# A two-layer hybrid transformer on one core: buffering of the modulation weights, a call's delay before their dots, and the place of one operand of a seven-product matrix multiplication

## The chip, the core and the metric

The kernel runs on one core of one Trainium2 chip. Five engines of the core work side by side: TensorE (PE; its weight loads are PEld), VectorE (DVE), ScalarE (ACT), GpSimd (POOL) and SyncE (SP), which here issues nearly all DMAs. Each engine takes its own instructions in order and waits at semaphores for the others. The metric is the device time of one execution in microseconds (us); below 1 us, nanoseconds (ns) are used.

## The reference

There are two streams of 256 tokens with 1024 channels, `h_lat` and `h_ctx`, and two layers. A layer is a half feed-forward block (ffn), a mixer (attention in layer 0, an mLSTM in layer 1), and a second ffn. What scales, shifts and gates each block comes from two conditioning vectors `c` and `c_ctx`, through a 1024 x 9216 matrix in each layer:

```python
def half_ffn(h, shift, scale, gate, w_in, w_out, g, b):
    xm = modulate(h, shift, scale)
    a, u = jnp.split(xm @ w_in, 2, axis=-1)
    y = (jax.nn.silu(a) * u) @ w_out
    return post_norm(h, 0.5 * gate * y, g, b)
...
    for i in range(DEPTH):
        mod_lat = jnp.split((jax.nn.silu(c) @ ada_w[i] + ada_b[i])[:, None, :], N_MOD, axis=-1)
        mod_ctx = jnp.split((jax.nn.silu(c_ctx) @ ada_w[i] + ada_b[i])[None, None, :], N_MOD, axis=-1)
        h_lat = half_ffn(h_lat, mod_lat[0], mod_lat[1], mod_lat[2], ffn_w_in[i, 0], ffn_w_out[i, 0], ln_g[i, 0], ln_b[i, 0])
        h_ctx = half_ffn(h_ctx, mod_ctx[0], mod_ctx[1], mod_ctx[2], ffn_w_in[i, 0], ffn_w_out[i, 0], ln_g[i, 0], ln_b[i, 0])
...
```

`w_in` is 1024 x 5632 and `w_out` is 2816 x 1024, all in float32. The last layer needs only `h_lat` after its mixer.

## The kernel before

**Precision.** A float32 operand x is split into a high part (ACT copies it to the type fp32r) and a low part (DVE subtracts the high part from x); `split` (L221) issues the two. A product is then three matmuls (`mm3`, L236): high by high, high by low, low by high. The stationary operand (weights) is 128 x 128; the moving operand (tokens) has 256 or 512 columns.

**An ffn** (`ffn`, L658) has two halves of 11 units each. An in-unit j (`unit_in`, or `fast_in` where the cheap form is used) multiplies all tokens by 128 columns of the `a` half of `w_in` and 128 of its `u` half; `ffn_g` (L547) makes silu(a)*u (an ACT Silu, L568, and a DVE product, L569) and splits it. After a half's units come the out-units d (`unit_out`, L681): eight of 33 matmuls with 512 columns in half 0, then four more such and four split by stream (the tail) in half 1; each ends in DVE additions to h (L692). The first four units (LEAD) of an ffn are done stream by stream with 256 columns. Weights arrive by SP's queue into three `raw` buffers (L206, issue at L207) and are split into one of seven `w` buffers (`pair`, L210), each 2 x 1024 values and 64 more, so that the pair may be shifted by `sh` values.

**The cheap form.** In the second half (hf 1) of the two middle ffns, (layer 0, second) and (layer 1, first), `fast_in` (L606) does a unit by seven half-size products instead of eight (a Winograd-Strassen scheme over the 2 x 2 blocks of the weights and of the two token streams). The seven products are a11, a12, s1, s2, a22, s4, s3, each of 12 matmuls with 256 columns: 84 matmuls a unit, 924 for the 11 units. Three sums of tokens, `made[0]`, `made[1]`, `made[2]`, are made beforehand by `fast_sums` (L579) after out-units 4 and 5 of half 0. They stand in one tile (`fast_operands`, L572): `made[0]` and `made[1]` at multiples of 1024 values, and `made[2]` pushed by FLIP = 56 values (224 bytes), so that it does not begin on a multiple of 64 values (256 bytes). All weights of the cheap form stand at SH = 16 values past such a multiple. Only the product a22 (L646) reads `made[2]`.

**The modulation matrix** is taken in pieces of 128 output columns, (layer, dt), dt = 0 to 71, 512 KB each. `ada_load` (L327) sends a piece to one of two `ada` buffers (SP, L331); `ada_dot` (L334) multiplies it by a conditioning vector and sums, a DVE instruction over 128 x 1024 (L337). A piece takes one dot for each stream that needs it: two for pieces 0 to 39 of layer 1, one for 40 to 71. `ada` (L343) does the load and then its dots. The 72 pieces of layer 1 are spread over the two middle ffns: `side` (L1598) gives the ffn functions to call after units, and `some(n)` (L1604) takes pieces until n dots are covered. `DOTS` (L91) says how many: in ffn (0, 1) four dots after each in-unit of half 0, three after out-units 0 to 3 of half 0, two after those of half 1; in ffn (1, 0) three, two and three. The calls of the four LEAD units come together after the fourth (L717). Dots are pinned (`pin`, L406): pinned instructions of an engine keep the order of the program among themselves, as do the two residual steps (L543) after every in-unit. Everything else on an engine is ordered by the scheduler that builds the program, earliest code first.

**Pools.** The ada buffers and the two silu'd conditioning vectors (`cb`) live in a pool `cp` at the right end of SBUF, opened by `silu_all`. Before out-unit 4 of half 0 (SUMSAT, L739) the pool is closed and its place given to the pool `st` with the token sums; after the last cheap unit `st` is closed and a new `cp` opened (L736).

Of the kernel before, what the change touches and what calls it, by code (L numbers as in the profile page):

```python
# [9 lines left out]
F32 = mybir.dt.float32  # L10
F32R = mybir.dt.float32r
# [7 lines left out]
P = 128  # L19
# [3 lines left out]
TL = 256  # L23
# [4 lines left out]
NFH = 11  # L28
# [3 lines left out]
BLOCK = 64  # L32

SH = 16
# [9 lines left out]
WB = 7  # L44
# [43 lines left out]

SUMSAT = 4
FLIP = 56  # L90
DOTS = {  # L91
    1: {("in",): 4, ("out", 0): 3, ("out", 1): 2},
    2: {("in",): 3, ("out", 0): 2, ("out", 1): 3},
}

TAILSTEP = {(0, 3, 1): 'bmccccccc', (1, 0, 2): 'c', (1, 0, 6): 'v', (1, 1, 7): 'rxxxxxxxx'}
# [73 lines left out]
class Body:  # L170
# [98 lines left out]
    def setup(self):  # L269
        nc, a = self.nc, self.a  # L270
        self.cols = col = self.t([P, 3 * BLOCK // 2])
        for i, x in enumerate((1.0, 1.0 / D, 1.0 / (D - P), 0.5 / D)):
            nc.vector.memset(col[:, i : i + 1], x)
        self.mean1, self.half = col[:, 1:2], col[:, 3:4]
        self.ones, self.mean, self.most = (col[:, i : i + 1].broadcast_to([P, P]) for i in range(3))

        self.h = self.t([P, ND, T])
        self.xh = self.t([P, ND, T + BLOCK], F32R)
        self.xl = self.t([P, ND, T + BLOCK], F32R)
        self.ident = self.t([P, P])  # L280
        self.vec = self.t([P, V_N])
        self.mod = {}
        self.s1 = {}

    def silu_c(self):

# [40 lines left out]
    def ada_load(self, layer, dt):  # L327
        if (layer, dt // ND) not in self.mod:
            self.mod[layer, dt // ND] = self.t([P, 2, ND])
        r = self.t([P, 1024], tag="ada", bufs=2, pool=self.cp)  # L330
        self.nc.sync.dma_start(r, self.a["ada_w"][layer, dt])  # L331
        return r

# [9 lines left out]
    def ada(self, layer, dt, vecs=(0, 1)):  # L343
        r = self.ada_load(layer, dt)
        for v in vecs:
            self.ada_dot(r, layer, dt, v)

    def modv(self):
        return self.t([P, 2, ND], tag="modv", bufs=12)
# [222 lines left out]
    def fast_operands(self, st):  # L572

        n = ND // 2 * TL
        x = self.t([P, 6 * n + FLIP], F32R, pool=st)
        at = [2 * i * n + (FLIP if i == 2 else 0) for i in range(3)]
        self.made = [[x[:, a + p * n : a + (p + 1) * n].rearrange("p (k f) -> p k f", f=TL) for p in range(2)] for a in at]

    def fast_sums(self, i):  # L579

# [22 lines left out]
        V.scalar_tensor_tensor(d, a, -1.0, d, ALU.mult, ALU.subtract)  # L603
        self.split(d, *made(2))

    def fast_in(self, j, w_in, st):  # L606

        nc, V, S = self.nc, self.nc.vector, self.nc.scalar
        half = 4 * P
        r0, r1 = (self.raw(w_in[2 * j + i]) for i in range(2))  # L610
        sums = self.t([P, 4 * half], tag="sums", bufs=1, pool=st)
        part = lambda x, i: x[:, i * half : (i + 1) * half]
        a11, a21, a12, a22 = part(r0, 0), part(r0, 1), part(r1, 0), part(r1, 1)
        s1, s2, s4, s3 = (part(sums, i) for i in range(4))
        add = lambda o, x, y: V.tensor_tensor(out=o, in0=x, in1=y, op=ALU.add)  # L615
        ws = [self.pair(sh=SH, n=half)] + [self.pair(sh=SH) for _ in range(3)]
        self.split(a11, *ws[0])
        self.split(r1, *ws[1])
        add(s1, a21, a22)
        add(s2, s1, a11)  # L620
        self.split(sums[:, : 2 * half], *ws[2])
        add(s4, s2, a12)
        add(s3, a11, a21)
        self.split(sums[:, 2 * half :], *ws[3])
        w = {n: [part(x, i) for x in ws[p]] for n, p, i in (
            ("a11", 0, 0), ("a12", 1, 0), ("a22", 1, 1), ("s1", 2, 0), ("s2", 2, 1), ("s4", 3, 0), ("s3", 3, 1),
        )}
        of = lambda k0, g: lambda k: self.x(k0 + k, g)
        made = lambda i: lambda k: [x[:, k, :] for x in self.made[i]]

        def product(o, name, x, first, last):
            for k in range(ND // 2):
                c = slice(k * P, (k + 1) * P)
                self.mm3(o, [y[:, c] for y in w[name]], x(k), first and k == 0, last and k == ND // 2 - 1, group=False)

        x, yv, z = self.mm()[:, :TL], self.mm(), self.mm()[:, :TL]
        y, v = yv[:, :TL], yv[:, TL:]
        a, u = self.tmp(), self.tmp()
        product(x, "a11", of(0, LAT), True, False)
        S.copy(a[:, :TL], x)  # L640
        product(y, "a12", of(ND // 2, LAT), True, True)
        product(v, "s1", of(0, CTX), True, False)
        S.copy(u[:, TL:], v)
        product(x, "s2", made(0), False, False)
        S.copy(a[:, TL:], x)
        product(z, "a22", made(2), True, True)  # L646
        S.copy(u[:, :TL], z)
        product(v, "s4", of(ND // 2, CTX), False, True)
        V.tensor_tensor(out=a, in0=a, in1=yv, op=ALU.add)
        S.activation(a, a, AF.Silu)  # L650
        product(x, "s3", made(1), False, True)
        u2 = u.rearrange("p (n f) -> p n f", n=2)
        V.scalar_tensor_tensor(u2, x[:, None, :].broadcast_to([P, 2, TL]), -1.0, u2, ALU.mult, ALU.subtract)
        V.tensor_tensor(out=a, in0=a, in1=u, op=ALU.mult)
        gh, gl = self.gt[j] = tuple(self.t([P, self.gw], F32R, tag=k, bufs=self.gn, pool=self.gp) for k in ("gh", "gl"))
        self.split(a, gh, gl)

    def ffn(self, layer, s, gate, groups, side, start=None, cpool=None):  # L658
# [4 lines left out]
        with self.tc.tile_pool(name=f"ffn{li}", bufs=1) as gp:  # L663
# [34 lines left out]
            for hf in range(2):  # L698
# [21 lines left out]
                fast = cpool is not None and hf == 1  # L720
                for j in js:
                    if fast:
                        self.fast_in(j, w_in, st)
                        continue
                    unit_in(j, stream(j), allg)
                    assert not self.running
                    if j >= LEAD + FAFTER:
                        self.fine = False
                    call("in", j)
                    self.residual(2, self.pin)  # L730
# [6 lines left out]
                    cpool = self.silu_all()  # L737
                for d in range(body):
                    if cpool and not hf and d == SUMSAT:  # L739
                        cpool.close()  # L740
                        self.n += 1
                        more = ExitStack()
# [837 lines left out]
def emit(ctx, tc, a, out):  # L1580
# [8 lines left out]
    made = {}  # L1589
# [8 lines left out]
    def side(key, coef, keep=(True, True), nxt=True, alone=False, dots={}):  # L1598
# [3 lines left out]
                    b.ada(*queue.pop(0))  # L1602

        def some(n):  # L1604
            while n > 0 and later:
                n -= len(later[0][2])
                b.ada(*later.pop(0))

        get = once(key, coef)

        b.begin = lambda g: b.norm(g, get, keep[0 if g == LAT else 1], nxt, alone)
        s = {}
        for j in range(NF):
            s["in", j] = (lambda: some(dots["in",])) if dots else pop
        for d in range(ND):
            s["out", 0, d] = (lambda d=d: some(dots["out", 0] if d < SUMSAT else 0)) if dots else pop
            s["out", 1, d] = lambda: some(dots.get(("out", 1), 0))
        return s

    both = (LAT, CTX)  # L1620
# [5 lines left out]
    cpool = b.ffn(0, 1, once("g1", lambda: b.half_gate(0, 8)), both, side("n2", lambda: b.ln_mod(0, 2, (1, 0)), dots=DOTS[1]), cpool=cpool)  # L1626
    cpool = b.ffn(1, 0, once("g2", lambda: b.half_gate(1, 2)), both, side("n3", lambda: b.ln_mod(1, 0, (1, 3)), (True, False), dots=DOTS[2]), cpool=cpool)
    assert not later, len(later)
    cpool.close()
    b.mlstm(lambda: b.shift_(1, 5, slice(0, 1)), side("n4", lambda: b.ln_mod(1, 1, (1, 6), 1), alone=True))  # L1630
    b.ffn_last(1, once("g3", lambda: b.half_gate(1, 8, 1)))
# [93 lines left out]
```

## Time and profile before

| | |
|---|---|
| Runs shown: median (lowest to highest) | 1651.09 us (1650.75 to 1655.48) |
| Profiled execution: its own time | 1649.32 us |
| Profiled execution: first to last instruction | 1647.6 us |
| Mean granted TensorE clock | 0.993 |
| DMA packets | 252.59 MB, mean 153 GB/s |
| ACT busy | 744.2 us (45%) |

A page of the profile lists the busy time of the engines, the span in 40 equal slices (of 41.2 us; a digit is a share in tenths), queues, the chain that ended last, and the costliest groups. Other views of the same trace: "waits" (who waited for whom: us in total, times, longest), "timeline" (instructions in order, runs of alike ones merged; in brackets the idle time before and what ended it), "groups by form" (one shape of one line: busy us, mean ns, idle before), and "windows" (a stretch of the span: its length, then for each engine the busy us and the number of instructions that touch it, the granted clock PEclk, the DMA share and rate). "SPq" is the issue of a DMA. L numbers are lines of the kernel. In "windows" the matmuls that run into a border count on both sides, so a row of 48 matmuls shows 49 to 51.

### The profile page before, as it was taken

The numbers are of one execution on the slowest core, as the hardware profiler recorded it, in microseconds if no ns is written. First come the engines' busy times: TensorE is split into PE (matmuls) and PEld (weight loads), VectorE is DVE, ScalarE is ACT, GpSimd is POOL, SyncE is SP. The second block draws the span as 40 slices with busy tenths as digits, with TensorE's granted clock in tenths as the row PEclk, the third lists the DMA queues.
The fourth block names the chain that finished last, engine by engine and source line by source line (L and its number), as shares of the span: only waits on it lengthen the run. The fifth ranks groups of instructions, "written<-read, shape, count | busy, mean of one in ns | idle before, by whom it ended". The sixth has DMA issues, their size and how long they took to land. (4 is left out here: it accounts for less than half of the span.)

```text
span 1647.6 us, 26587 instructions
## 1 busy us (share of the span) xinstructions
PE 1617.8 (98%) x10308; PEld 1457.4 (88%) x10308; DVE 1353.8 (82%) x2689; ACT 744.2 (45%) x1269; POOL 61.6 (4%) x76
## 2 busy tenths in 40 slices
PE   9999999999999999999999999899999999999998
PEld 6888888899988998889999998689999989999987
DVE  5899978649888879999977977799965968897687
ACT  5532222314676343425652433225652656656542
POOL 0000000001011200000000100000000100020000
PEclk9999999999999999999999999899999999999999
DMA  9577765622103247733353267733352342437652
GB/s 371 187 237 231 239 215 187 203 76 84 65 1 91 64 143 229 229 128 129 103 182 126 78 193 255 250 120 116 115 155 66 116 120 78 135 109 256 181 172 96
DMA packets 72495, 252.59 MB, mean 153 GB/s; under 512 B 7984, under 2 KB 10800, under 8 KB 72368
## 3 DMA queue, kind: packets, MB, share of 16 engines
q1 hardware_dynamic: 71792, 250.10, 47.8%
q8 instruction: 81, 1.33, 0.3%
q10 hardware_dynamic: 576, 0.79, 0.1%
q14 instruction: 46, 0.38, 0.1%
HBM read 249.81 MB, written 1.05 MB: 152 GB/s over the span
## 5 line engine op out<-in xcount | busy, mean ns | idle before, releaser
L238 PE MATMUL t<-t,t 128*128 128x256 f32 (+2 forms) x8412 | 1325.1, 319 | 14.2 <-ACT t L222 10.7
L238 PEld LDWEIGHTS t<-t,t 128*128 128x128 f32 x8412 | 1193.1, 189 | 133.9 <-ACT t L222 12.7
L222 ACT CAST t<-t 128x1024 fp32r<-128x1024 f32 (+3 forms) x521 | 429.6, 844 | 467.3 <-PE t L238 244.3
L227 DVE TENSOR_TENSOR t<-t,t 128x256 fp32r<-128x256 f32 (+2 forms) x740 | 514.7, 728 | 116.6 <-ACT t L222 112.5
L337 DVE SCALAR_TENSOR_TENSOR t<-t,t 128x1024 bf16<-128x1024 f32 x224 | 263.5, 1220 | 25.2 <-DMA t<-in_ada_w 24.5
L909 PE MATMUL t<-t,t 128*128 128x256 f32 (+1 forms) x256 | 79.5, 311 | 0.0
L911 PE MATMUL t<-t,t 128*128 128x256 f32 (+1 forms) x256 | 78.8, 308 | 0.0
L910 PE MATMUL t<-t,t 128*128 128x256 f32 (+1 forms) x256 | 78.4, 306 | 0.0
L568 ACT ACTIVATE t<-t 128x512 f32<-128x512 f32 (+1 forms) x71 | 34.3, 487 | 95.6 <-PE t L238 95.6
L692 DVE SCALAR_TENSOR_TENSOR t<-t,t,t 128x256 f32<-128x256 f32 x96 | 42.7, 478 | 37.0 <-PE t L238 37.0
L569 DVE TENSOR_TENSOR t<-t,t 128x512 f32<-128x512 f32 (+1 forms) x71 | 38.9, 551 | 32.8 <-PE t L238 26.7
L464 POOL TENSOR_TENSOR t<-t,t 128x256 f32<-128x256 f32 x30 | 23.4, 781 | 1130.9 <-ACT t L454 1129.7
L1424 PE MATMUL t<-t,t 128*128 128x512 f32 (+3 forms) x286 | 60.2, 365 | 2.0 <-ACT t L1501 1.0
L837 PE MATMUL t<-t,t 128*128 128x512 f32 (+1 forms) x300 | 60.7, 364 | 0.0
L1424 PEld LDWEIGHTS t<-t,t 128*128 128x128 f32 (+2 forms) x286 | 43.8, 159 | 18.3 <-issue 2.2
L837 PEld LDWEIGHTS t<-t,t 128*128 128x128 f32 x300 | 51.4, 189 | 9.1 <-DVE t L831 0.3
L454 ACT ACTIVATE t<-t 128x256 f32<-128x256 f32 x72 | 26.2, 411 | 72.3 <-DVE t L447 72.3
L544 ACT ACTIVATE t<-t,t 128x256 f32<-128x256 f32 x64 | 29.4, 503 | 57.4 <-DVE t L543 57.4
L909 PEld LDWEIGHTS t<-t,t 128*128 128x128 f32 x256 | 48.4, 189 | 2.7
L910 PEld LDWEIGHTS t<-t,t 128*128 128x128 f32 x256 | 48.2, 188 | 2.6
L911 PEld LDWEIGHTS t<-t,t 128*128 128x128 f32 x256 | 48.1, 188 | 2.5
L615 DVE TENSOR_TENSOR t<-t,t 128x512 f32<-128x512 f32 x66 | 45.3, 686 | 1.1 <-DMA t<-in_ffn_in 0.3
(200 smaller groups left out, 1065.5 us busy)
## 6 DMA issues: line engine op xcount, KB each, us to landing
t<-in_ffn_in SPq DMA_DIRECT2D x168, 512.0 KB, 4.1
t<-in_ada_w SPq DMA_DIRECT2D x137, 512.0 KB, 4.2
t<-in_ffn_out SPq DMA_DIRECT2D x66, 512.0 KB, 4.4
t<-in_ffn_last SPq DMA_DIRECT2D x22, 512.0 KB, 3.5
t<-in_att_in SPq DMA_DIRECT2D x12, 512.0 KB, 3.5
t<-in_c SPq DMA_DIRECT2D x8, 512.0 KB, 7.8
t<-in_att_out SPq DMA_DIRECT2D x8, 512.0 KB, 3.5
t<-in_ml_qk SPq DMA_DIRECT2D x8, 512.0 KB, 3.6
```

The source lines that it names most:

```text
L222: self.behind(self.nc.scalar.copy(h, x))
L227: self.behind(self.nc.vector.tensor_tensor(out=ls, in0=xs, in1=hs.bitcast(F32), op=ALU.subtract))
L238: mm = lambda *k, **kw: self.nc.tensor.matmul(*k, skip_group_check=not group, **kw)
L337: ins = nc.vector.scalar_tensor_tensor(self.tmp().bitcast(BF16), r, 1.0, self.cb[:, v, :], ALU.mult, ALU.mult, accum_out=to)
L569: V.tensor_tensor(out=sl, in0=sl, in1=pu[:, :n], op=ALU.mult)
L615: add = lambda o, x, y: V.tensor_tensor(out=o, in0=x, in1=y, op=ALU.add)
L692: V.scalar_tensor_tensor(z, y[:, gg[0] - t0 : gg[1] - t0], gate()[:, v, d : d + 1], z, ALU.mult, ALU.add)
L837: pin(nc.tensor.matmul(o, gs[g], ws[k][w][:, i : i + n], start=k == k0 and g == w == 0, stop=k == k1 - 1 and g == 1,))
L909: mm(o, self.xh[:, k, c], wh, start=k == 0, stop=False)
L910: mm(o, self.xh[:, k, c], wl, start=False, stop=False)
L911: mm(o, self.xl[:, k, c], wh, start=False, stop=k == ND - 1)
L1424: mm = lambda *k, **kw: pin(nc.tensor.matmul(*k, **kw))
```

## The change

Three parts.

First, pieces and dots: four ada buffers (PIECES) instead of two. `some(n)` now counts pieces and not dots; it first does the dots of the pieces that the call before loaded (`flush`), and then only issues the loads of n further pieces. What is left is flushed before the pool is closed at SUMSAT, and after ffn (1, 0). `DOTS` lists pieces for each call. For ffn (0, 1): two after each in-unit, 2, 2, 1, 1 after out-units 0 to 3 of half 0, one each in half 1: 32 pieces. For ffn (1, 0): two after in-units 0 to 3, three after 4 to 8, two after 9 and 10, two after out-units 0 to 2 of half 0, and 2, 2, 2, 1 after those of half 1: 40 pieces. Before, the counts came out as 34 and 38, with none in half 1 of ffn (1, 0).

Second, `made[2]` stands at 4096 values in the tile, a multiple of 64; the 56 values are kept as a tile of their own.

Third, in the first cheap unit (j = 11) alone one product reads an operand beside that line. In ffn (0, 1), ACT copies both parts of `made[2]` into a `w` buffer at 56 values, and a22 reads the copies. In ffn (1, 0), the weights of a11 stand at TURN = 24 values instead of 16.

```diff
+TURN = 24
+PIECES = 4
 DOTS = {
-    1: {("in",): 4, ("out", 0): 3, ("out", 1): 2},
-    2: {("in",): 3, ("out", 0): 2, ("out", 1): 3},
+    1: {**{("in", j): 2 for j in range(11)}, **{("out", 0, d): 2 if d < 2 else 1 for d in range(4)}, **{("out", 1, d): 1 for d in range(4)}},
+    2: {**{("in", j): 2 for j in range(4)}, **{("in", j): 3 if j < 9 else 2 for j in range(4, 11)}, **{("out", 0, d): 2 if d < 3 else 0 for d in range(4)},
+        **{("out", 1, d): 2 if d < 3 else 1 for d in range(4)}},
 }
...
-        r = self.t([P, 1024], tag="ada", bufs=2, pool=self.cp)
+        r = self.t([P, 1024], tag="ada", bufs=PIECES, pool=self.cp)
...
+    def flush(self):
+
+        while self.waiting:
+            r, layer, dt, vecs = self.waiting.pop(0)
+            for v in vecs:
+                self.ada_dot(r, layer, dt, v)
...
-        x = self.t([P, 6 * n + FLIP], F32R, pool=st)
-        at = [2 * i * n + (FLIP if i == 2 else 0) for i in range(3)]
-        self.made = [[x[:, a + p * n : a + (p + 1) * n].rearrange("p (k f) -> p k f", f=TL) for p in range(2)] for a in at]
+        x = self.t([P, 6 * n], F32R, pool=st)
+        self.t([P, FLIP], pool=st)
+        self.made = [[x[:, (2 * i + p) * n : (2 * i + p + 1) * n].rearrange("p (k f) -> p k f", f=TL) for p in range(2)] for i in range(3)]
...
-    def fast_in(self, j, w_in, st):
+    def fast_in(self, j, w_in, st, first):
...
+        t4 = self.made[2]
+        if j == NFH and first == "x":
+            w = self.t([P, 2 * 1024 + BLOCK], F32R, tag="w", bufs=WB)
+            t4 = [w[:, FLIP + i * 1024 : FLIP + (i + 1) * 1024].rearrange("p (k f) -> p k f", f=TL) for i in range(2)]
+            for i in range(2):
+                S.copy(t4[i], self.made[2][i].bitcast(F32))
...
-        ws = [self.pair(sh=SH, n=half)] + [self.pair(sh=SH) for _ in range(3)]
+        ws = [self.pair(sh=TURN if j == NFH and first == "w" else SH, n=half)] + [self.pair(sh=SH) for _ in range(3)]
...
-        product(z, "a22", made(2), True, True)
+        product(z, "a22", lambda k: [x[:, k, :] for x in t4], True, True)
...
-                        self.fast_in(j, w_in, st)
+                        self.fast_in(j, w_in, st, "w" if layer else "x")
...
                     if cpool and not hf and d == SUMSAT:
+                        self.flush()
                         cpool.close()
...
         def some(n):
-            while n > 0 and later:
-                n -= len(later[0][2])
-                b.ada(*later.pop(0))
+            b.flush()
+            for _ in range(min(n, len(later))):
+                layer, dt, vecs = later.pop(0)
+                b.waiting.append((b.ada_load(layer, dt), layer, dt, vecs))
...
     assert not later, len(later)
+    b.flush()
     cpool.close()
```

More of the change, by code (lines that the diff above doesn't have):

```diff
@@ L283, in setup @@
         self.s1 = {}
+        self.waiting = []
     def silu_c(self):
@@ L1613, in side @@
         for j in range(NF):
[L1614 removed]
+            s["in", j] = (lambda j=j: some(dots.get(("in", j), 0))) if dots else pop
         for d in range(ND):
[L1616 to L1617 removed]
+            s["out", 0, d] = (lambda d=d: some(dots.get(("out", 0, d), 0))) if dots else pop
+            s["out", 1, d] = lambda d=d: some(dots.get(("out", 1, d), 0))
         return s
```

## The prediction

> **What bounds the kernel now.** I began with the page: busy shares and the 40 slices.
>
> ```profile
> span 1647.6 us, 26587 instructions
> ...
> PE 1617.8 (98%) x10308; PEld 1457.4 (88%) x10308; DVE 1353.8 (82%) x2689; ACT 744.2 (45%) x1269; POOL 61.6 (4%) x76
> ...
> PE   9999999999999999999999999899999999999998
> ...
> PEclk9999999999999999999999999899999999999999
> ```
>
> PE is busy nearly throughout, so time is won only where PE waits, where its clock falls, or where its matmuls follow each other more slowly than they could. One slice shows 8 for both PE and its clock: the 26th, 1030 to 1071 us, where ffn (1, 0) passes from its in-units to its out-units. The windows view there, for PE alone, with borders at the starts of groups of 48 matmuls:
>
> ```profile
> 1031.92:1042.80 10.88, 10.88 (x49) 1.00 0.87 289
> 1042.80:1064.03 21.23, 13.68 (x50) 0.76 0.67 223
> 1064.03:1074.91 10.88, 10.88 (x50) 1.00 0.85 260
> 1049.80:1057.20 7.40, 0.00 (x0) 0.66 0.80 269
> 1052.20:1057.30 5.10, 0.00 (x0) 0.50 0.79 272
> 1057.31:1062.38 5.07, 5.07 (x11) 0.50 0.51 181
> ```
>
> The same 48 matmuls take 10.88 us before and after, and 21.23 us in between: 10.35 us lost. The last three rows split it: PE stands still for over 7.4 us, and works at clock 0.50 until 1062.4. What was it waiting for? The timeline, all engines:
>
> ```profile
> 1042.81 1.22 DVE L337 SCALAR_TENSOR_TENSOR t<-t,t 128x1024 bf16<-128x1024 f32 x1 [2.75 <-DMA t<-in_ada_w]
> ...
> 1043.96 0.87 DVE L543 SCALAR_TENSOR_TENSOR t<-t,t,t 128x256 f32<-128x256 f32 x2
> ...
> 1044.76 0.68 DVE L569 TENSOR_TENSOR t<-t,t 128x512 f32<-128x512 f32 x1
> ...
> 1049.25 1.22 DVE L337 SCALAR_TENSOR_TENSOR t<-t,t 128x1024 bf16<-128x1024 f32 x1
> ...
> 1049.36 1.47 SPq L331 DMA_DIRECT2D t<-in_ada_w  x2
> ...
> 1053.98 1.23 DVE L337 SCALAR_TENSOR_TENSOR t<-t,t 128x1024 bf16<-128x1024 f32 x1 [2.37 <-DMA t<-in_ada_w]
> ...
> 1055.13 0.88 DVE L543 SCALAR_TENSOR_TENSOR t<-t,t,t 128x256 f32<-128x256 f32 x2
> ...
> 1055.93 0.68 DVE L569 TENSOR_TENSOR t<-t,t 128x512 f32<-128x512 f32 x1
> ...
> 1056.64 1.56 ACT L222 CAST t<-t 128x512 fp32r<-128x512 f32 x2
> ...
> 1057.31 6.88 PE L238 MATMUL t<-t,t 128*128 128x512 f32 x18 [7.55 <-ACT t L222]
> ```
>
> Read it backwards. PE needs the split result of in-unit 10. Its DVE product (L569, at 1055.93) stands behind the pinned residuals (L543) and dots of in-unit 9, whose third dot sat 2.37 us waiting for a piece. That load could go only when the first dot had freed one of two buffers (L331 at 1049.36). From one L543 to the next is 11.17 us, and PE's unit takes 10.88: DVE never catches up. The group of all dots on DVE in 966.6:1055.9; the waits of DVE in 590:750 and of SP's queue in 966:1056; and the page's row of the loads:
>
> ```profile
> L337 DVE SCALAR_TENSOR_TENSOR t<-t,t 128x1024 bf16<-128x1024 f32 x33 | 39.6, 1222 | 15.0 <-DMA t<-in_ada_w 14.9
> ...
> DVE t L337 <- DMA t<-in_ada_w: 1.7, 3, 1.0
> ...
> SPq L331 <- DVE t L337: 39.7, 26, 3.5
> ...
> t<-in_ada_w SPq DMA_DIRECT2D x137, 512.0 KB, 4.2
> ```
>
> **Part one: pieces, buffers, delay.** It removes no dot: 33 run on DVE up to the product of unit 10. With the new counts, two come from the piece left by ffn (0, 1), twelve from calls 0 to 2, four from call 3, fifteen from calls 4 to 8: 33 again. What goes is their waiting. A load now has a whole call, the time of a unit, for its landing of 4.2 us. Without the 14.9 us, the product of unit 10 would come at 1055.93 - 14.9 = 1041.0, before its matmuls end: units start at 966.6 (row below), and seven of 10.88 end at 1042.8. PE needs the result 30 matmuls later, 1042.8 + 30 x 10.88/48 = 1049.6. About half of the 14.9 must go for the stall to vanish; I count on nearly all. **Gain 10.35 us**, bounds 0 and 10.35. DMAs have room for it:
>
> ```profile
> 966.60:1049.40 82.80, 82.80 (x368) 68.56 (x366) 65.96 (x109) 27.03 (x40) 0.00 (x0) 1.00 0.75 245
> ```
>
> In ffn (0, 1) only 1.7 us of such waiting exists and PE does not stand still there: nothing. The DMA issues of pieces stay on SP in the same order between the weights'; an L331 that waits holds the weights behind it, as now (39.7 us), with two more buffers before it must.
>
> The clock's share can be separated. From 1057.31 to 1062.38 PE worked at 0.50, so about half of 5.07 us, 2.5 us of the 10.35, went with the clock. The Trainium skill ("TensorE: Matmul & The Clock Gate", Part 1) has the gate fall after an idle window of some 3.4 us and prices it as throttled time x (1 - K/N). The rows agree on the fall (0.50 within the stall), but by that formula the 10.2 us at half clock would cost 5.1, and the rows say half of it, because PE stood still for the first half.
>
> New work: seven dots of ffn (1, 0) move into half 1, where there were none. Six fall where DVE has room, the seventh (`flush` after the ffn) does not:
>
> ```profile
> 1235.00:1262.00 27.00, 27.00 (x169) 24.40 (x168) 10.64 (x28) 3.15 (x3) 0.00 (x0) 1.00 0.26 81
> ...
> 1276.00:1301.00 25.00, 24.10 (x207) 23.63 (x206) 24.81 (x74) 14.26 (x30) 6.12 (x8) 1.00 0.27 83
> ...
> 1308.43 11.78 PE L238 MATMUL t<-t,t 128*128 128x256 f32 x77 [0.46 <-ACT t L521]
> ...
> L222 ACT CAST t<-t 128x1024 fp32r<-128x1024 f32 x309 | 323.3, 1050 | 355.3 <-PE t L238 227.3 <-issue 70.4 <-DMA t<-in_ffn_in 20.3
> ...
> L337 DVE SCALAR_TENSOR_TENSOR t<-t,t 128x1024 bf16<-128x1024 f32 x224 | 263.5, 1220 | 25.2 <-DMA t<-in_ada_w 24.5
> ```
>
> DVE is the third pair: 10.64 of 27.00 busy, then 24.81 of 25.00. Being pinned, the seventh dot lands in or near the full stretch, ahead of the norm's last steps, which PE awaits at 1308.43. **Cost 1.1 us**: a dot of 1.22 less its overlap with the next (1053.98 to 1055.13 is 1.15). Bounds 0 and 1.2.
>
> **Parts two and three: the place of one operand.** The windows of the two cheap stretches (924 matmuls each), the first unit of the first, and 48 matmuls (a11 to s2) of the second unit and of the third of ffn (1, 0):
>
> ```profile
> 747.19:854.70 107.51, 107.36 (x926) 107.14 (x925) 98.67 (x130) 66.11 (x109) 0.00 (x0) 1.00 0.40 124
> 1112.98:1220.22 107.24, 107.24 (x925) 107.23 (x924) 96.03 (x127) 65.69 (x108) 0.00 (x0) 1.00 0.40 119
> 747.19:757.07 9.88, 9.88 (x86) 9.87 (x84) 9.06 (x14) 5.71 (x9) 0.00 (x0) 1.00 0.44 163
> 1122.79:1128.23 5.44, 5.44 (x51) 5.44 (x49) 5.35 (x9) 3.78 (x6) 0.00 (x0) 1.00 0.45 166
> 1132.46:1138.12 5.66, 5.66 (x51) 5.66 (x50) 5.53 (x8) 3.78 (x6) 0.00 (x0) 1.00 0.57 180
> ```
>
> Same code, shapes and clock, and no stall, yet 5.44 against 5.66 us: matmuls follow each other in 113.3 or 117.9 ns. PE keeps a pace until something turns it, and what lies between these two rows is one a22, the one product off the 256-byte line. So each a22 turns the pace, and units alternate. All 924 at 113.3 would take 104.7; the stretches lose 2.8 and 2.5 us. After the change one product turns the pace once, out of the slow one in which ffn (0, 1) begins, and nothing turns it back. In ffn (0, 1) the first unit stays as it is (9.88 against 84 x 0.1133 = 9.52, 0.36 lost), which leaves 2.4 to win. In ffn (1, 0) a11 does it at once: tokens at 0 and weights at 24 stand to each other, modulo 64, as tokens at 56 and weights at 16 do (-24 and 40), so I take it that a11 turns the pace as a22 did; 2.4 to win.
>
> Against it in ffn (0, 1) stand the two copies. They are nearest to the ACT row of 128x1024 above: 2 x 1.05 us. ACT has room over the stretch (66 of 107.5 us), but the copies wait for the last token sums, just before the first unit, where DVE is full and already brings a result late:
>
> ```profile
> 735.00:747.19 12.19, 12.19 (x56) 10.09 (x55) 12.19 (x19) 4.48 (x7) 0.00 (x0) 1.00 0.13 41
> 762.51:764.23 1.72, 1.57 (x14) 1.36 (x13) 1.29 (x3) 1.72 (x4) 0.00 (x0) 1.00 0.27 24
> ```
>
> The second row is an a22 of 12 matmuls that takes 1.72 us for 1.4, with ACT full: PE waits behind ACT. I leave those 0.3 us in and add 0.7 for the copies (0 if DVE comes early, 2.1 if both stand before what PE needs). **Gain 1.4 + 2.4 = 3.8 us.** Bounds: everything at 113.3 and no cost, 4.8 gained; everything at 117.9 (924 x 0.1179 = 108.9) plus the copies, 1.4 + 1.7 + 2.1 = 5.2 lost.
>
> **Sum** against the profiled execution: 1649.32 - 10.35 + 1.1 - 3.8 = 1636.3. It ran 1.8 us under the median 1651.09; half of that I take as the stall's own variation, half I add: **1637.0**.
>
> **Rivals.** (1) The place does nothing, or the pace is set by something else (a wait, the entry), and both stretches stay slow: 1637.0 + 3.8 = 1640.8 without effect, 1644 slow. For it: two stretches only, and TURN has no row. Against: the alternation above. The Trainium skill speaks for this rival: the same page (Part 2, "Step-by-step") gives PE two independent read ports, so that a weight load takes nothing from the running matmul, and a pace of N/2.4 + 2.5 ns, with no word on addresses. The rows, 113.3 and 117.9 for one N, disagree.
>
> (2) The stall shrinks but stays: pieces still arrive late, as SP reaches their loads late behind waiting weights. With a third of the 14.9 us removed, 5 us of the stall go, and the rest (2.5) falls short of the clock's fall: 1637.0 + 2.5 = 1639.5; with nothing removed, 1647.
>
> (3) Slower: SP's queue. Three pieces are loaded a call while three wait, so two of three loads stand at SP until the previous call's dots have run; behind them stand the next unit's two weight loads. If DVE stays a unit late, these come late too, and PE waits in every unit instead of once. It decides once the loads slip by more than the 10.35 + 2.7 us in total over seven units, 1.9 each; at 2.5 each the time is 1649.3 + 17.5 - 13 = 1654. For it: the 39.7 us that SP waits now. Against: the added buffers shorten those waits.
>
> (4) It changes nothing that counts: DVE, now on time, runs into another wait before the out-units, or later stretches return the gain: 1650.
>
> **How the numbers follow.** Forecast 0.52, rival 1 0.20, rival 2 0.12, rival 3 0.09, rival 4 0.07. The range 1632 to 1646 holds the forecast (1632 if the copies and the seventh dot cost nothing and the offset is absent: 1649.3 - 15.2 = 1634, less 2 for relief elsewhere), rival 1 and most of rival 2. About 0.3%, 5 us, is what a measurement of this kernel can tell from no change: faster is the forecast, rival 1 and most of rival 2 (0.82), same the rest of it and most of rival 4 (0.08), slower the remainder (0.10).
>
> **What would show it.** Right: no PE wait near 1050 and one dip of the clock fewer; DVE's waiting for pieces down from 14.9 to under 4 us there; both cheap stretches near 105 us with 5.44 in every row of four products after the first unit; PE's wait near the end of ffn (1, 0) longer by a dot. Wrong: a stall left at that passage, 5.66 in all units of a stretch, or SP's issues of weights late against PE.

## The result and the profile after

| | before | after |
|---|---|---|
| Median (lowest to highest) | 1650.75 us (1649.79 to 1655.48) | 1641.71 us (1641.26 to 1643.87) |
| Ratio of the times, 95% interval | | 0.9945 (0.9929 to 0.9961) |
| Profiled execution, own time | 1649.32 us | 1641.71 us |

The change makes the kernel 9.0 us faster by the medians; 14 were forecast from 1651.09 to 1637.0. The page after, in the lines that were shown of before; for the group of dots the last column is DVE's idle time ahead of them:

```profile
span 1639.9 us, 26579 instructions
...
PE 1616.3 (99%) x10308; PEld 1453.8 (89%) x10308; DVE 1351.6 (82%) x2689; ACT 746.6 (46%) x1271; POOL 62.0 (4%) x76
...
PE   9999999999999999999999999999999999999998
...
PEclk9999999999999999999999999999999999999999
...
L341 DVE SCALAR_TENSOR_TENSOR t<-t,t 128x1024 bf16<-128x1024 f32 x224 | 260.7, 1220 | 0.0
```

The 8 in the 26th slice is gone from PE and from its clock, and the 25.2 us in which DVE sat idle before its dots are 0.0. So the stall of ffn (1, 0) and its cause have gone. The rest stands in the windows: the 48 matmuls where the stall was, the first cheap stretch with its first, second and seventh unit, the second cheap stretch, the 110 us behind it with the seventh dot, and 192 matmuls with 256 columns in the last ffn.

```profile
1042.36:1053.24 10.88, 10.88 (x50) 9.01 (x49) 9.71 (x15) 3.61 (x6) 0.00 (x0) 1.00 0.66 229
747.05:855.14 108.09, 106.81 (x925) 105.58 (x924) 95.09 (x127) 65.36 (x109) 0.00 (x0) 1.00 0.38 116
747.05:756.85 9.80, 9.80 (x86) 9.80 (x84) 8.16 (x13) 6.08 (x10) 0.00 (x0) 1.00 0.38 117
756.85:766.37 9.52, 9.52 (x87) 9.52 (x85) 8.40 (x12) 6.02 (x10) 0.00 (x0) 1.00 0.33 112
804.58:814.60 10.02, 9.79 (x86) 9.59 (x85) 8.90 (x13) 5.87 (x11) 0.00 (x0) 1.00 0.37 108
1102.20:1211.02 108.82, 108.82 (x925) 108.82 (x924) 96.04 (x131) 65.94 (x109) 0.00 (x0) 1.00 0.38 118
1211.02:1321.91 110.89, 109.89 (x736) 100.28 (x734) 88.21 (x220) 51.94 (x81) 8.87 (x12) 1.00 0.40 131
1476.81:1499.42 22.61, 22.61 (x194) 22.61 (x193) 19.03 (x31) 15.82 (x23) 0.00 (x0) 1.00 0.88 273
```

The same two last stretches of matmuls, in the windows of before:

```profile
1220.22:1331.38 111.16, 109.49 (x736) 100.22 (x734) 80.88 (x205) 52.13 (x82) 8.80 (x12) 1.00 0.34 107
1485.97:1507.73 21.76, 21.76 (x195) 21.76 (x194) 18.53 (x30) 15.03 (x22) 0.00 (x0) 1.00 0.86 286
```

Set against before, row by row: the stall's 48 matmuls 21.23 to 10.88, 10.35 won; first cheap stretch 107.51 to 108.09, 0.58 lost; second 107.24 to 108.82, 1.58 lost; the part with the seventh dot 111.16 to 110.89, 0.27 won; the last ffn's 192 matmuls 21.76 to 22.61, 0.85 lost. Together 7.6 us, which is what lies between the two profiled executions (1649.32 - 1641.71). What lies outside these rows cancels: 1.0 us more is won ahead of the second cheap stretch, and 1.0 us is lost behind the part with the seventh dot.

Three things were not foreseen. In the second cheap stretch PE is busy without a break, and 108.82 us for 924 matmuls is 117.8 ns each: the slow pace from end to end, so TURN = 24 turned nothing. In the first the pace did turn (9.80 us for the first unit, 9.52 for the second, which is 84 matmuls of 113.3 ns), but the sixth unit takes 9.65 us, those after it 10.02 to 10.04 and the last 10.43, with PE no longer busy throughout. And the 256-column run of the last ffn, which the change doesn't touch, ran at the slow pace in this execution.

What PE waits for in the late units is in the timeline of after. The unit shown is the seventh, from 804.58; at the fast pace its fifth product would end 5 x 1.36 us later, at 811.4:

```profile
806.15 0.68 DVE L666 TENSOR_TENSOR t<-t,t 128x512 f32<-128x512 f32 x1
806.75 1.22 DVE L230 TENSOR_TENSOR t<-t,t 128x1024 fp32r<-128x1024 f32 x1
...
807.88 0.68 DVE L670 SCALAR_TENSOR_TENSOR t<-t,t 128x512 f32<-128x512 f32 x1
808.49 0.68 DVE L632 TENSOR_TENSOR t<-t,t 128x512 f32<-128x512 f32 x1
809.09 0.68 DVE L671 TENSOR_TENSOR t<-t,t 128x512 f32<-128x512 f32 x1
...
809.80 1.65 ACT L225 CAST t<-t 128x512 fp32r<-128x512 f32 x2 [1.98 <-DVE t L671]
...
811.36 0.36 ACT L660 COPY t<-t 128x256 f32<-128x256 f32 x1
...
811.77 0.50 PE L241 MATMUL t<-t,t 128*128 128x256 f32 x2 [0.23 <-ACT t L660]
```

Product s4 adds to the sum that L660 must first copy out (the result of s1). That copy stands in ACT's queue behind casts (L225) that wait 1.98 us for DVE's last step of the previous unit (L671); and on DVE L671 stands behind a split (L230) and a sum (L632) of the next unit's weights. So it comes 4.5 us after the start of the unit, and the copy starts at 6.8 us, just when PE wants s4. Whether that order of the two queues was always there, or came with the change, is what experiments 6, 7 and 10 ask.

### The profile page after: what moved, and what is told of

It reads as the page before. It is cut to its first block, busy times and chain, and to the rows that moved or that the text cites. A ratio compares the mean times of both kernels' runs of the same rounds, so it can differ in the third digit from the quotient of the medians.

```text
span 1639.9 us, 26579 instructions
## 1 busy us (share of the span) xinstructions
PE 1616.3 (99%) x10308; PEld 1453.8 (89%) x10308; DVE 1351.6 (82%) x2689; ACT 746.6 (46%) x1271; POOL 62.0 (4%) x76
## 3 DMA queue, kind: packets, MB, share of 16 engines
HBM read 249.81 MB, written 1.05 MB: 153 GB/s over the span
## 5 line engine op out<-in xcount | busy, mean ns | idle before, releaser
L225 ACT CAST t<-t 128x1024 fp32r<-128x1024 f32 (+3 forms) x521 | 428.2, 843 | 507.6 <-PE t L241 205.2
L230 DVE TENSOR_TENSOR t<-t,t 128x256 fp32r<-128x256 f32 (+2 forms) x740 | 513.9, 729 | 124.4 <-ACT t L225 121.7
L632 DVE TENSOR_TENSOR t<-t,t 128x512 f32<-128x512 f32 x66 | 45.3, 686 | 0.3
L532 ACT ACTIVATE t<-t,t 128x256 fp32r<-128x256 f32 x72 | 32.8, 503 | 27.4 <-DVE t L531 27.4
```

The lines of the kernel that those rows point to most:

```text
L225: self.behind(self.nc.scalar.copy(h, x))
L230: self.behind(self.nc.vector.tensor_tensor(out=ls, in0=xs, in1=hs.bitcast(F32), op=ALU.subtract))
```

## The experiments

They ask in turn what part one is worth alone (1, 5), what turns the pace (2, 3, 4, 6), where the late waits come from (2, 7, 10), what the seventh dot costs (8), and how little is enough (9). Each expectation names the theories that it tells apart. Times of before measured beside them: 1650.85 us for experiments 1 to 4, 1650.99 for 5 to 8, 1651.91 for 9 and 10. Experiments 2, 3, 4, 7 and 10 are a single execution each; they are read by their stretches, and their times alone show little.

### 1. Part one alone

`made[2]` at 56 values again, no copies, no TURN; pieces, buffers and delay as after:

```diff
-        x = self.t([P, 6 * n], F32R, pool=st)
-        self.t([P, FLIP], pool=st)
...
+        x = self.t([P, 6 * n + FLIP], F32R, pool=st)
+        at = [2 * i * n + (FLIP if i == 2 else 0) for i in range(3)]
...
-                        self.fast_in(j, w_in, st, "w" if layer else "x")
+                        self.fast_in(j, w_in, st, "")
```

> Pieces, buffers and delay as in the changed kernel, but the third token sum off the 256-byte line in every cheap unit as before, no copies, no TURN. Theory A (the stall at 1050 us is worth some 10.4 us, and the two parts about the operand's place cost 0.6 + 1.6 us in the cheap stretches): faster than the changed kernel by about 2 us, so near 1639.5 us; no PE wait near 1050; the two cheap stretches back at 107.5 and 107.2 us with units alternating between 9.9 and 9.7 us. Rival (the stretches are long because DVE, now on time, or the buffers of the pieces disturb them): the stretches stay at 108 to 109 us and the time at 1641.7 us.

1639.92 us, ratio 0.9929 (0.9915 to 0.9942). Its two cheap stretches in the windows:

```profile
747.03:854.26 107.23, 107.23 (x925) 107.23 (x924) 97.02 (x127) 65.66 (x109) 0.00 (x0) 1.00 0.38 120
1101.13:1208.36 107.23, 107.23 (x925) 107.23 (x924) 95.92 (x131) 66.06 (x109) 0.00 (x0) 1.00 0.38 119
```

Theory A held. Part one alone does all the good. The units alternate between the paces as they did before, 107.23 us in both stretches against 108.09 and 108.82 after, so by the traces it does 2.45 us more there than the whole change; the intervals of the two ratios overlap. Dots that come on time don't spoil the pace.

### 2. The copies in both stretches

ACT's copies of `made[2]` at 56 values for a22 in ffn (1, 0) too, in place of TURN:

```diff
-                        self.fast_in(j, w_in, st, "w" if layer else "x")
+                        self.fast_in(j, w_in, st, "x")
```

> The changed kernel with the copies beside the line in the first cheap unit of both stretches, and no TURN. Theory A (a product whose tokens stand beside the line turns the pace; TURN on the weights does not; the copies' use of a w buffer gives DVE and ACT an order that needs 10.03 us a unit): in ffn (1, 0) the pace turns in the first unit to 5.44 us for four products, and after about five units PE waits some 0.5 us in each unit; the stretch takes 108 us against 108.8. Rival 1 (the pace of that stretch can't be turned): 5.66 us throughout, 108.8 us. Rival 2 (the late units of ffn (0, 1) wait for something of that ffn alone): turned and no waits, 105.2 us.

1643.34 us. The second stretch, its first and its second unit in the windows:

```profile
1104.22:1212.40 108.18, 107.09 (x926) 105.86 (x924) 92.98 (x126) 65.21 (x109) 0.00 (x0) 1.00 0.38 115
1104.22:1114.02 9.80, 9.80 (x85) 9.80 (x84) 6.39 (x12) 6.08 (x11) 0.00 (x0) 1.00 0.35 107
1114.02:1123.54 9.52, 9.52 (x86) 9.52 (x85) 8.40 (x12) 6.12 (x10) 0.00 (x0) 1.00 0.36 112
```

The pace of ffn (1, 0) does turn, in the first unit, when the operand at 56 is the tokens. And the waits, with PE busy 107.09 of 108.18 us, now stand in this stretch too. They follow the copies.

### 3. Eleven places for the weights of a11

One place in each unit of the first stretch, the same ones in reverse in the second; no copies:

```diff
+SWEEP = (24, 8, 32, 40, 48, 56, 0, 12, 20, 28, 4)
...
-        ws = [self.pair(sh=TURN if j == NFH and first == "w" else SH, n=half)] + [self.pair(sh=SH) for _ in range(3)]
+        ws = [self.pair(sh=SWEEP[j - NFH if not first else NF - 1 - j], n=half)] + [self.pair(sh=SH) for _ in range(3)]
...
```

> No copies; every cheap unit has the weights of a11 at another place: 24, 8, 32, 40, 48, 56, 0, 12, 20, 28, 4 values in the units of ffn (0, 1), the same list from its end in ffn (1, 0); all other weights at 16, all tokens on the line. Theory A (only the tokens' place, or the distance to the tokens in a direction that 24 does not give, turns the pace): no unit turns, 9.9 us each, or only some places other than 24. Rival (TURN failed only since a11 is the first product after the 512-column matmuls): 24 turns the pace where it stands in the tenth or eleventh unit, so that products go from 1.41 to 1.36 us within that unit.

1636.63 us. Units 1, 3, 7 and 9 of the first stretch (places 24, 32, 0 and 20):

```profile
746.82:756.71 9.89, 9.89 (x86) 9.89 (x84) 9.22 (x14) 5.19 (x9) 0.00 (x0) 1.00 0.32 108
766.61:776.22 9.61, 9.61 (x86) 9.61 (x85) 9.61 (x13) 5.90 (x10) 0.00 (x0) 1.00 0.40 117
804.89:814.81 9.92, 9.92 (x87) 9.92 (x85) 9.21 (x14) 5.99 (x10) 0.00 (x0) 1.00 0.36 121
824.71:834.30 9.59, 9.59 (x86) 9.59 (x85) 8.97 (x13) 6.00 (x10) 0.00 (x0) 1.00 0.39 111
```

A unit of 9.9 us is slow throughout (84 x 117.8 = 9.90), one of 9.6 is fast after its a11. Place 24 at the entry leaves the pace slow here as well, and in the last unit of the second stretch it leaves a fast pace fast: where it was tried it did nothing. Turned from slow to fast: 32 and 20 here, 4 and 56 in the second stretch. 0 turned from fast to slow in both. 8 and 12 left the pace as it was, either way; 28, 40 and 48 were met only in the fast pace and kept it. 32, 20, 4 and 56 were met once in the fast pace too, and left it fast, where the tokens at 56 of before turn it both ways. So the place acts, and the entry is no obstacle to it (4 turns there). But it doesn't act by the distance between the two operands modulo 64 as the prediction reckoned it. Why just these places act isn't shown.

### 4. One matmul more

To see whether the place acts by itself or through the time that the a11 with it takes, one extra matmul of n columns, whose result isn't used, behind a11; n differs by unit, no operand off its usual place:

```diff
+EXTRA = (128, 64, 32, 256, 192, 96, 16, 160, 224, 48, 8)
...
+        more = EXTRA[j - NFH if not first else NF - 1 - j]
+        nc.tensor.matmul(zz[:, TL : TL + more], w["a11"][0][:, :P], self.x(0, LAT)[0][:, :more], start=True, stop=True, skip_group_check=True)
...
```

> No copies, no TURN, all tokens on the line; one additional matmul stands between a11 and a12 in each cheap unit, into unused columns, with 128, 64, 32, 256, 192, 96, 16, 160, 224, 48, 8 columns in ffn (0, 1) and the list from its end in ffn (1, 0). Theory A (the pace is a phase between weight loads and matmuls that any step of another length can shift): some lengths turn the pace from 1.41 to 1.36 us a product from a12 on, others leave it. Rival (only the operand's place matters): no unit turns and every product takes 1.41 us, with 0.02 to 0.12 us more for the additional matmul.

1642.76 us. The last five products (60 matmuls) of four units: behind 192 columns in the first and the second stretch, and behind 32 in the first and the second.

```profile
790.41:797.21 6.80, 6.80 (x62) 6.80 (x61) 6.20 (x10) 3.30 (x7) 0.00 (x0) 1.00 0.13 29
1167.00:1174.07 7.07, 7.07 (x62) 7.07 (x61) 6.29 (x10) 3.26 (x7) 0.00 (x0) 1.00 0.13 31
770.42:777.49 7.07, 7.07 (x63) 7.07 (x62) 6.43 (x10) 3.26 (x7) 0.00 (x0) 1.00 0.20 61
1186.99:1193.79 6.80, 6.80 (x62) 6.80 (x61) 6.21 (x10) 3.29 (x7) 0.00 (x0) 1.00 0.14 45
```

A matmul of another length turns the pace too: from slow to fast with 128 columns in both stretches, from fast to slow with 48, 64 and 96 in both. But 8, 16, 32, 192 and 224 did it in one stretch only, and each pair of rows above shows the same length with both results. The pace looks like a phase that an irregular step can shift; which step shifts it where is not settled by this run.

### 5. Four buffers alone

The kernel before with one number changed:

```diff
-        r = self.t([P, 1024], tag="ada", bufs=2, pool=self.cp)
+        r = self.t([P, 1024], tag="ada", bufs=4, pool=self.cp)
```

> The kernel before with four ada buffers instead of two; counts, places and the dots right behind their loads as before. Theory A (the dots wait because the third piece of a call finds no free buffer): with four buffers a load goes a call earlier even without the delay, DVE's waiting for pieces in ffn (1, 0) falls from 14.9 to under 4 us, PE no longer stands still near 1050 us, and the time is that of pieces, buffers and delay together, 1640 us. Rival (the delay is what counts, since a load is still issued in the same call as its dots): at least half of the waiting stays, PE still stands still for 2 to 7 us, time 1643 to 1650 us.

1638.69 us, ratio 0.9923 (0.9907 to 0.9938). The page's group of dots:

```profile
L337 DVE SCALAR_TENSOR_TENSOR t<-t,t 128x1024 bf16<-128x1024 f32 x224 | 260.7, 1223 | 0.0
```

The two more buffers do it: no dot waits for a piece, and PE's waits between 930 and 1110 us come to 0.6 us, none of them for a split result. Neither the call's delay nor the new counts add anything that the times can tell (experiment 1 has both, and its interval overlaps).

### 6. Turned by weights at 4 values

After without the copies; a11's weights at 4 values in the first unit of both stretches:

```diff
-TURN = 24
+TURN = 4
...
-                        self.fast_in(j, w_in, st, "w" if layer else "x")
+                        self.fast_in(j, w_in, st, "w")
```

> The changed kernel without copies, the weights of a11 in the first cheap unit of both stretches at 4 values instead of 16 (TURN = 4), all tokens on the line. Theory A (place 4 turns the pace; the order of DVE and ACT that comes without the copies keeps up with 9.52 us a unit): both stretches at 5.44 us for four products from the first unit on, no PE waits in them, 104.8 to 105.5 us each; time 1641.7 - 3 - 3.7 = about 1635 us, faster than the kernel with the pieces alone by 4 us. Rival 1 (DVE and ACT fall behind 9.52 us in any order): waits of PE appear in the late units as in the changed kernel, the stretches take 107 to 108 us. Rival 2 (place 4 does not turn the pace at the entry of a stretch): 108.8 us in one or both.

1635.35 us, ratio 0.9906 (0.9889 to 0.9922). The stretches in the windows:

```profile
747.66:852.44 104.78, 104.78 (x925) 104.78 (x924) 96.92 (x127) 65.51 (x109) 0.00 (x0) 1.00 0.39 122
1100.36:1205.14 104.78, 104.78 (x925) 104.78 (x924) 96.01 (x131) 65.96 (x109) 0.00 (x0) 1.00 0.40 122
```

This is the 105 us that the prediction expected of both: one product turns the pace, nothing turns it back, and PE never waits, so the fast pace by itself does not outrun DVE and ACT. Its timeline, for the steps shown of after, in a unit that starts at 795.32:

```profile
795.59 0.68 DVE L666 TENSOR_TENSOR t<-t,t 128x512 f32<-128x512 f32 x1
...
796.19 0.69 DVE L670 SCALAR_TENSOR_TENSOR t<-t,t 128x512 f32<-128x512 f32 x1
...
796.79 1.22 DVE L230 TENSOR_TENSOR t<-t,t 128x1024 fp32r<-128x1024 f32 x1
...
797.92 0.69 DVE L671 TENSOR_TENSOR t<-t,t 128x512 f32<-128x512 f32 x1
...
798.64 0.62 ACT L225 CAST t<-t 128x512 fp32r<-128x512 f32 x1 [0.34 <-DVE t L671]
799.60 0.37 ACT L660 COPY t<-t 128x256 f32<-128x256 f32 x1 [0.34 <-PE t L241]
```

Here L670 comes straight after L666 and only one split stands ahead of L671, which comes 2.6 us into the unit and not 4.5; ACT's copy then waits for PE, and not PE for the copy. So the scheduler has ordered the two queues otherwise in this kernel than in after.

### 7. The turn by weights, with copies that a22 reads

As 6, and a22 of the first unit reads copies as after, but on a multiple of 64 values, so that they turn nothing:

```diff
-        if j == NFH and first == "x":
+        if j == NFH:
...
-            t4 = [w[:, FLIP + i * 1024 : FLIP + (i + 1) * 1024].rearrange("p (k f) -> p k f", f=TL) for i in range(2)]
+            t4 = [w[:, i * 1024 : (i + 1) * 1024].rearrange("p (k f) -> p k f", f=TL) for i in range(2)]
```

> As the kernel with TURN = 4 in both first cheap units, but there a22 reads copies of the third token sum that stand in a w buffer on the 256-byte line. Theory A (holding a w buffer until a22 of the first unit leaves DVE and ACT in an order that takes 10.03 us a unit, whatever the place): pace 5.44 us from the start, then PE waits of about 0.5 us in every unit from the fifth or sixth on, 107.5 to 108.2 us a stretch. Rival (the late units wait because of the operand's place or of the turned pace): as with TURN = 4 alone, 105 us and no waits.

1640.18 us. The stretches:

```profile
746.78:854.77 107.99, 106.91 (x925) 105.74 (x924) 94.98 (x127) 65.33 (x109) 0.00 (x0) 1.00 0.36 116
1102.67:1210.63 107.96, 106.84 (x926) 105.78 (x924) 93.27 (x126) 65.09 (x109) 0.00 (x0) 1.00 0.38 115
```

With the fast pace from the second product on, 3.2 us more a stretch than in 6. The place of the copies is cleared; making them, or having a22 read them and so keeping their buffer, is the cost. The waits turn the pace as well. In the second stretch, the first four products of the seventh unit, right behind the first waits (those of the eighth take 5.44 us again):

```profile
1160.15:1165.80 5.65, 5.65 (x50) 5.65 (x49) 5.65 (x9) 2.85 (x6) 0.00 (x0) 1.00 0.24 89
```

### 8. The seventh dot moved

As 6, with one piece more after in-unit 9 and none after the last out-unit, so that no dot follows ffn (1, 0):

```diff
-    2: {**{("in", j): 2 for j in range(4)}, **{("in", j): 3 if j < 9 else 2 for j in range(4, 11)}, **{("out", 0, d): 2 if d < 3 else 0 for d in range(4)},
-        **{("out", 1, d): 2 if d < 3 else 1 for d in range(4)}},
+    2: {**{("in", j): 2 for j in range(4)}, **{("in", j): 3 if j < 10 else 2 for j in range(4, 11)}, **{("out", 0, d): 2 if d < 3 else 0 for d in range(4)},
+        **{("out", 1, d): 2 if d < 3 else 0 for d in range(4)}},
```

> The kernel with TURN = 4 in both first cheap units, and the last piece taken after in-unit 9 of ffn (1, 0) instead of after its out-unit 3 of half 1, so that no dot runs behind the ffn. Theory (the seventh dot costs 1.1 us on the chain through DVE at the end of ffn (1, 0)): faster by about 1.1 us than with TURN = 4 alone, all of it between 1260 and 1310 us. Rival (the dot lies in a gap of DVE): the same within 0.3 us there.

1634.71 us, ratio 0.9900 (0.9885 to 0.9915): 0.6 us from experiment 6, with overlapping intervals. The same matmuls behind the second stretch, in 6 and then here:

```profile
1205.14:1316.49 111.35, 110.04 (x736) 100.50 (x735) 88.67 (x221) 52.26 (x82) 8.90 (x12) 1.00 0.39 132
1203.49:1314.71 111.22, 110.29 (x736) 100.96 (x735) 88.13 (x219) 52.38 (x83) 8.89 (x12) 1.00 0.41 135
```

They differ by 0.13 us, within the 0.3 of the rival, so the dot costs next to nothing. It isn't for the rival's reason, though: in the timeline of 6 the dot runs from 1272.53 with DVE work right before and right behind it, in no gap. That PE doesn't come to wait a dot's length longer is seen; why not is open.

### 9. The least that does it

The kernel before with four buffers, `made[2]` on the line, and a11's weights at 4 values in the first cheap unit; no delay, old counts, no copies:

```diff
+TURN = 4
...
-        r = self.t([P, 1024], tag="ada", bufs=2, pool=self.cp)
+        r = self.t([P, 1024], tag="ada", bufs=4, pool=self.cp)
...
-        ws = [self.pair(sh=SH, n=half)] + [self.pair(sh=SH) for _ in range(3)]
+        ws = [self.pair(sh=TURN if j == NFH else SH, n=half)] + [self.pair(sh=SH) for _ in range(3)]
```

> The kernel before with three edits only: four buffers for the pieces, the third token sum on the line, and the weights of a11 in the first cheap unit of both stretches at 4 values from the line. Neither the call's delay, nor the new counts, nor the copies. Theory A (the buffers alone remove the stall, and 4 is a turning place for the weights): no wait of PE near 1050 us, both cheap stretches 104.8 us, time 1634 to 1637, the same as e6_turn_by_weights (1635.35). Rival: with a faster first stretch the dots, which here run in the call that loads them, come late again (DVE's two units per dot are as before), PE waits at the passage from in-units to out-units of ffn (1, 0), and the time is 1638 to 1643.

1634.22 us (1633.67 to 1635.30), ratio 0.9896 (0.9879 to 0.9912). Both stretches take 104.78 us and no dot waits. It is 17.7 us faster than before, and with three small edits as fast as experiment 6 with the whole of part one.

### 10. The copies made and not held

As 7, but a22 reads the token sum itself, so that nothing reads the copies and their buffer comes free at once:

```diff
-        product(z, "a22", lambda k: [x[:, k, :] for x in t4], True, True)
+        product(z, "a22", made(2), True, True)
```

> As e7_copies_on_the_line, with the copies still made by ACT ahead of the first unit of both stretches (2 copies of 128x1024), but read by nothing: a22 reads the token sum itself, and the buffer of the w ring comes free at once. Theory A (the late waits come from the order that DVE and ACT take when the ring is a buffer short until a22): both stretches 104.8 to 105.4 us, no wait of PE from unit 6 on, time 1634 to 1637. Rival (it is ACT's work for the copies that puts the two engines behind, and they never catch up): both stretches about 108 us with the waits from unit 6, time about 1640.

1633.75 us. The copies stand at 56 values here, as in after, which nothing reads. The first stretch in the windows:

```profile
747.15:851.93 104.78, 104.78 (x926) 104.78 (x924) 97.63 (x129) 65.91 (x108) 0.00 (x0) 1.00 0.39 123
```

ACT's waits over 45 us of late units, in after and then here:

```profile
ACT t L225 <- DVE t L671: 7.9, 4, 2.0
ACT t L225 <- DVE t L632: 5.4, 4, 1.4
```

```profile
ACT t L225 <- PE t L241: 7.0, 5, 1.4
ACT t L662 <- PE t L241: 4.9, 5, 1.0
ACT t L660 <- PE t L241: 2.4, 5, 0.5
...
ACT t L225 <- DVE t L671: 0.5, 3, 0.2
```

The copies' work costs nothing. With them made but not read, ACT is early and waits for PE; where a22 of the first unit reads them, ACT waits for DVE, 13.3 us in four units, and PE for it. So what costs is that a22 reads the copies. The likely reason is that one of seven `w` buffers is then missing until a22 has run. Its lack shows ahead of the first unit, where the fifth cast of weights in a row has to wait for matmuls in 7 (and 1.86 us in after), and only for its own load here. From the timelines of 7 and then here:

```profile
746.98 1.05 ACT L225 CAST t<-t 128x1024 fp32r<-128x1024 f32 x1 [1.87 <-PE t L241]
```

```profile
745.74 1.05 ACT L225 CAST t<-t 128x1024 fp32r<-128x1024 f32 x1 [0.26 <-DMA t<-in_ffn_in]
```

That the build-time order of DVE and ACT settles in the worse pattern for all later units because of this is argued and not shown: a22 also depends on ACT's copies there, and no run has the one without the other.

## Why the prediction held, and where it failed

Forecast 1637.0, measured 1641.71: the sign and the range held, but the gain was 9.0 us and not 14, and its parts were not those of the sum. The range held by the stall alone: parts two and three, which were to win 3.8 us, lost 2.2 (0.58 and 1.58).

**The stall: right.** 10.35 us forecast, 10.35 found, with DVE's waiting for pieces at 0.0. The mechanism given (the first dot frees one of two buffers too late) is shown by experiment 5. Only the credit was wrong: "a load now has a whole call" isn't needed, two more buffers are. The clock went with it: 1.00 over the rows where before had 0.50. The Trainium skill ("TensorE: Matmul & The Clock Gate", Part 1) has the clock fall after an idle window of about 3.4 us. At this passage the trace agrees on the fall (with the standstill of over 7.4 us there is one, without it none), but it came some 2.4 us into the standstill, by the prediction's own rows (0.66 over 1049.80:1057.20, 0.50 from 1052.20). And the clock fell without a standstill too. In this row of before PE is busy throughout at 0.50, and had waited no longer than 0.3 us at a time in the 11 us ahead; a run of 14 matmuls of one column lies across its start. Why the clock fell there is open.

```profile
1458.30:1461.70 3.40, 3.40 (x16) 0.50 0.48 178
```

**The second cheap stretch: the failed step.** 2.4 us were to be won and 1.58 were lost, 4.0 in all. The step was "tokens at 0 and weights at 24 stand to each other, modulo 64, as tokens at 56 and weights at 16 do (-24 and 40), so I take it that a11 turns the pace as a22 did". An equality that no row had shown carried half of part three. Weights at 24 turned nothing (after, experiment 3); weights at 4 do (6 and 9), where the stretch took 104.78 us.

**The first cheap stretch: right turn, mis-sized cover.** The copies at 56 turned the pace within the first unit, as said. At 9.80 us for it and ten of 9.52 the stretch would have taken 105.0; it took 108.09, so 3.1 us were lost to waits, where the sum had 0.3 for an a22 that waits and 0.7 for the copies, the latter with bounds of 0 to 2.1. The copies were priced as ACT's work, and that was indeed hidden (10). What was left out is what follows from a22 reading them (7): another order of two queues, most likely through the buffer that the copies keep. The bounds were drawn around the wrong quantity.

**The seventh dot: mis-sized.** 1.1 us, bounds 0 and 1.2; measured next to nothing, as the 110 us around it shrank by 0.27, and moving it gave 0.13 (8). The prediction was right that the dot lands where DVE is full, and wrong that PE would wait for the whole of it.

**What the sum didn't hold:** the last ffn's pace, 0.85 us lost in this execution by no edit near it. Added up from the sum of 1636.3: 2.0 for the first stretch (1.4 forecast, -0.6 found), 4.0 for the second, 0.85 for the last ffn, less 1.1 for the dot and 0.3 won there, make 1641.7, the profiled execution's own time. (The prediction adds half of 1.8 us to 1636.3 and writes 1637.0; it would be 1637.2.)

**The rivals.** Rival 1 (both stretches slow) was right of ffn (1, 0), but half of its reason falls: the place of an operand does act on the pace, though other steps act as well (4, 7). The page of the Trainium skill that spoke for it ("TensorE: Matmul & The Clock Gate", Part 2, "Step-by-step") has weight loads take nothing from a running matmul, with one pace for one N. The runs disagree: they have 117.8 ns and 113.4 (104.78 us / 924) for the same shapes, with one product's weights at 24 or at 4 values. Rivals 2 and 4 fall with the stall. Rival 2 had also taken 2.5 us of idleness to be too short for the clock to fall, which the 2.4 us above don't bear out. Rival 3 asked for weights late behind SP's loads; but there is no wait of PE at the passage, and those of the cheap stretch name ACT.

## What to carry to other kernels

Count what an added operation holds and who must wait for it, not only how long it runs: two copies of 1.05 us were hidden, but having a product read them, from a buffer of a ring, cost 3 us, as two other engines' queues came out in another order. Before a delay and a new schedule are written for late data, try the buffers alone: one number (2 to 4) gave 12 us here. And where a sum rests on two settings being equivalent, use the one that a row of the profile has shown to work, or price the other as unproven.

## What the runs showed of the hardware that was not expected

- **TensorE has two paces for one stream of 256-column matmuls**, 113.3 and 117.9 ns, and keeps the one it is in: over 900 in a row in experiments 6, 9 and 10. A single product with its weights at 4, 20, 32 or 56 values past a 256-byte multiple turned it from slow to fast and left it when fast; at 0 it turned it from fast to slow; 8, 12 and 24 did not act. All but 4 and 24 rest on one or two units.
- **An inserted matmul shifts it as well**, but 32 and 192 columns did so in one stretch and not in the other. A wait of PE shifted it too (7). What rule decides is open.
- **The pace of the last ffn differs between profiles** without any edit near it: the 192 matmuls take 21.76 us in seven of the twelve (before among them) and 22.61 in five (after among them). Whether one kernel does both is not shown, as each was profiled once. A comparison of single profiles carries about 1 us of this.
- **The clock can fall while PE works**: 0.50 for 3.4 us from 1458.30 in before, with no wait of PE over 0.3 us ahead of it. At this passage the profiles of experiments 5 and 9 show such a fall too, the other nine none.
